# Activation block sums of the feed-forward stage: one piece per product of chunk 1, the rest under the products down of chunk 0, each engine one step further apart

## The chip, the cores and the metric

One core of a Trainium2 chip runs the whole program in one launch. The metric is the device time of that launch in microseconds (us). The engines are TensorE (PE; PEld is its weight load), VectorE (DVE), ScalarE (ACT), GpSimd (POOL) and the sync engine (SP), which issues the DMAs here. Each engine takes its instructions in the order in which the program lists them and waits on semaphores for the others.

## What is computed

Two layers of an encoder, 1024 tokens by 1024 features, in float32. A layer is a mixer (two kinds of attention with gates) and a feed-forward part. Only the feed-forward part matters here:

```python
h = rmsnorm(x, pre_ffn_g[l]) @ w_ffn_up[l]       # 1024 -> 4096
f = jnp.square(jax.nn.relu(h)) @ w_ffn_down[l]   # 4096 -> 1024
x = x + rmsnorm(f, post_ffn_g[l])
```

## The kernel before, in words

**Split operands.** Every float32 operand of a large product is scaled by a power of two and split into a float16 high part and a float16 low part. A product is then three matmuls (high by high, high by low, low by high) that add up in PSUM. ACT makes a high part (a copy into float16) and DVE the low part (value minus high part).

**Chunks.** The 4096 hidden features are worked in 8 chunks of 512. Chunks 0 and 1 are multiplied up directly (`up_first`, `up`). Chunks 2 to 7 (`up7`) use a seven-product scheme for 2 by 2 blocks, which needs five sums or differences of blocks of the activations (`UB` lists seven operands, two of them plain blocks) and sums of blocks of the weights. `down` multiplies a chunk down and adds into `acc`.

**The activation sums.** `u_sums` is a Python generator. It makes the five block sums in two halves each, so ten pieces, numbered 0 to 9 here. One piece is: two additions of 128x1024 on POOL (`tt` with `G`) into a buffer of the pool "p", a third addition on DVE (`tt`), the high part on ACT (`act`) and the low part on DVE (`sub`). Each `next(usums)` is a step of a software pipeline: before the change, step n issues the low part of piece n-2, the third addition and the high part of piece n-1 and POOL's additions of piece n. The pool "p" (`wk()`) has 4 buffers; a sum holds one until its low part is done.

**The order around it.** The part is in a `manual_schedule`: for PE, DVE, ACT and POOL the order in the program is the order on the engine. `run` first makes the second halves of chunk 0 (`up_first(i, 1)`, one step after each of the four), then prepares the low and high parts of chunk 0's hidden values (`split`) and of its down weights (`down_weights`) as work in a queue that `up(1, 6)` takes from: six pieces of it (`adv`) after the matmuls of each of its four products. Before the change a step of `u_sums` stands after the first and after the fourth of these six, and what is left is issued after `up`.

In `up(1, 6)` the four products are called P0 to P3 here, 48 matmuls of 128x512 each. The queue gives: hidden norm (under P0); four high and four low parts of the hidden values and the first square of the down weights (P1); the other three squares and their sum, line 239 (P2); the high and low parts of the down weights (P3). A mark in the queue makes the sum's use, a one-column matmul with a matrix of ones (line 243), stand on PE in front of the next product:

```python
        def stat():

            if mark[0]:
                mark[0] = next(work[0]) == 2
```

`relu2` (two instructions on ACT) empties each product's PSUM; PSUM of this kind (A) has two buffers, so a product needs the one before last emptied.

Then `down(0, 2)` makes eight products of 24 matmuls, one for each block of 128 tokens (tb 0 to 7). After each, DVE empties PSUM into `acc`. Beside them run the head of chunk 2's weights (`up_head`: two DMAs, four squares on ACT that each take a "p" buffer, their sum at line 1287 and its matmul of ones at line 1291, in front of tb 3) and `flow()`, which makes weight sums for `up7(2)`: an addition on POOL into a "p" buffer, a high part on POOL, a low part on DVE.

All of this occurs once in each of the two layers.

Of the kernel before, what the change touches and what calls it, by code (L numbers as in the profile page):

```python
# [44 lines left out]
def tile_hybrid_encoder(  # L45
# [27 lines left out]
    def mt(shape, dt=F16):  # L73
        return sb.tile(shape, dt, tag="m", name=nm("m"), bufs=NM)
# [7 lines left out]
    def wk(shape=(128, 1024), dt=F32):  # L82
        return sb.tile(list(shape), dt, tag="p", name=nm("p"), bufs=NP)

    def gt(shape, dt=F32):
        return sb.tile(shape, dt, tag="g", name=nm("g"), bufs=NG)
# [10 lines left out]
    def lay(n):  # L97
        return sb.tile([128, 4], F32, tag="lay", name=nm("lay"), bufs=32)[:, :n]

    def psA(cols=1024):  # L100
        return ps.tile([128, 1024], F32, tag="A", name=nm("A"), bufs=2)[:, :cols]
# [16 lines left out]
    def ts(o, i, s1, op0, s2=None, op1=None, e=V):  # L118
        if op1 is None:
            e.tensor_scalar(out=o, in0=i, scalar1=s1, scalar2=None, op0=op0)  # L120
        else:
            e.tensor_scalar(out=o, in0=i, scalar1=s1, scalar2=s2, op0=op0, op1=op1)  # L122

    def tt(o, a, b, op, e=V):
        e.tensor_tensor(out=o, in0=a, in1=b, op=op)  # L125
# [4 lines left out]
    def sub(o, a, b, e=V):  # L130
        tt(o, a, b, ALU.subtract, e)
# [4 lines left out]
    def stt(o, a, s, b, op0, op1):  # L136
        V.scalar_tensor_tensor(out=o, in0=a, scalar=s, in1=b, op0=op0, op1=op1)  # L137

    def act(o, i, f=AF.Copy, **k):
        S.activation(o, i, f, **k)  # L140
# [1067 lines left out]
    def ffn(l, U, su_inv, wup0, nxt):  # L1208
# [24 lines left out]
        def u_sums():  # L1233

            homes = iter((gt, gt, ptt, mt, mt))
            items = []
            for i, (a, b, sg) in enumerate(UB):
                if b is None:
                    UC[i] = [[U[*a, e][:, k, :] for k in range(4)] for e in range(2)]
                    continue  # L1240
                home = next(homes)
                if home is gt:
                    t = [[gt([128, 2, 512], F16) for _ in range(2)] for e in range(2)]
                else:
                    full = [home([128, 4, 512]) for e in range(2)]
                    t = [[f[:, 2 * j : 2 * j + 2, :] for j in range(2)] for f in full]
                UC[i] = [[t[e][k // 2][:, k % 2, :] for k in range(4)] for e in range(2)]
                items += [(a, b, ALU.add if sg > 0 else ALU.subtract, t, j) for j in range(2)]
            yield 1
            n0 = len(items)  # L1250
            sums = {}
            for n in range(n0 + 2):
                if n > 1:
                    *_, t, j = items[n - 2]
                    sub(t[1][j], sums.pop(n - 2), t[0][j])
                if 0 < n <= n0:
                    a, b, op, t, j = items[n - 1]
                    ks = slice(2 * j, 2 * j + 2)
                    tt(sums[n - 1], sums[n - 1], U[*b, 1][:, ks, :], op)
                    act(t[0][j], sums[n - 1])  # L1260
                if n < n0:
                    a, b, op, t, j = items[n]
                    ks = slice(2 * j, 2 * j + 2)
                    sums[n] = wk((128, 2, 512))
                    tt(sums[n], U[*a, 0][:, ks, :], U[*b, 0][:, ks, :], op, G)
                    tt(sums[n], sums[n], U[*a, 1][:, ks, :], ALU.add, G)
                yield 1
# [113 lines left out]
        def up_mm(wu, b, f, pa, ths):  # L1381
            (wh,), (wl,) = wu[b][:2]
            for k in range(8):
                for (a, r) in ((0, 0), (0, 1), (1, 0)):
                    lw = (wh, wl)[a][:, k, f * 128 : (f + 1) * 128]
                    for i, th in enumerate(ths):
                        TE.matmul(pa[:, i * 512 : (i + 1) * 512], lw, U[k // 4, th, r][:, k % 4, :],  # L1387
                                  start=(k == 0 and a == 0 and r == 0), stop=(k == 7 and a == 1))

        def up_scale(wu, b):  # L1390
            c = lay(1)
            mul(c, wu[b][2], su_inv)
            return c

        def relu2(h, pa, c, o):
            act(h, pa, AF.Relu, scale=c)
            act(h, h, AF.Square, accum_out=o)
# [17 lines left out]
        def up(ch, n):  # L1415
            wu = wup.pop(ch)
            hf, hs = [], lay(4)
            st[ch] = hf, hs
            for b in range(2):
                c = up_scale(wu, b)  # L1420
                for f in range(2):
                    pa = psA()
                    stat()
                    up_mm(wu, b, f, pa, (0, 1))
                    for i in range(n):
                        adv(1)
                        if i in (0, 3):
                            next(usums, 0)
                    h = mt([128, 1024], F32)
                    relu2(h, pa, c, hs[:, b * 2 + f : b * 2 + f + 1])  # L1430
                    hf.append(h)
            drain()
# [43 lines left out]
        def down_factor(ch, inv):  # L1476
            c = lay(1)
            mul(c, wdn[ch][2], inv)
            wdn[ch].append(c)

        def split_and_weights(ch):

            dw = down_weights(ch, (ptt,) * 4, 2)
            next(dw)
            work.extend([split(ch), dw])
# [42 lines left out]
        def down(ch, n):  # L1528
            down_factor(ch, st.pop((ch, "inv")))
            for tb in range(8):  # L1530
                pa = psA()
                stat()
                down_mm(ch, tb, pa, True, True)
                adv(n)
                if ch < 5 and tb > 0:
                    flow()
                if ch == 0:
                    acc[tb] = mt([128, 1024], F32)
                    ts(acc[tb], pa, wdn[ch][4], ALU.mult)
                else:  # L1540
                    stt(acc[tb], pa, wdn[ch][4], acc[tb], ALU.mult, ALU.add)
            drain()
            if ch < 5:
                for _ in range(8):
                    flow()
            del st[ch], wdn[ch]
# [65 lines left out]
        def run():  # L1612
            nonlocal g_post, usums
            with tc.manual_schedule(engines=ENGINES):
                work.extend([up_weights(1, b, wt) for b in range(2)])
                usums = u_sums()
                for i in range(4):
                    up_first(i, 1)
                    next(usums)
                drain()  # L1620
                split_and_weights(0)
                up(1, 6)
                for _ in usums:
                    pass
                for ch in range(1, 6):
                    work.append(up_head(ch + 1))
                    down(ch - 1, 2)
                    if ch < 5:
                        split_and_weights(ch)
                        up7(ch + 1, (4, 4, 2, 2, 2, 3, 5))  # L1630
                work.append(up_head(7))
                up7(6, (2,) * 7)
                for _ in range(4):
                    flow()
                split_and_weights(5)
                up7(7, (4, 4, 2, 2, 2, 3, 5))
                work.append(last_work())
                down(5, LW)
                g_post = load_gain(post_ffn_g[l], D)
                if not lastl:  # L1640
                    work.append(nxt["start"]())
                for tb in range(7 if lastl else 8):
                    stat()
                    if tb > 2:
                        turn(tb - 3)
                    pa = psA()
                    for ch in (6, 7):
                        down_mm(ch, tb, pa, ch == 6, ch == 7)
                    adv(LA)
                    norms(tb)  # L1650
                    xs[tb] = wk()
                    SY.dma_start(out=xs[tb], in_=x1[l][tb * 128 : (tb + 1) * 128, :])
                    stt(acc[tb], pa, wdn[6][4], acc[tb], ALU.mult, ALU.add)
                    square(acc[tb], nv[tb][:, 0:1])
                    if lastl:
                        mul(acc[tb], acc[tb], g_post, G)
                drain()
                if lastl:
                    last_block()
# [15 lines left out]
        g_post, usums = None, None  # L1675
# [75 lines left out]
    for l in range(depth):  # L1751
        hold, wup0 = {}, [[], []]
        YA, ivA, YB, ivB = mixer(l, U, su_inv, b2u, w1, first if l == 0 else None, late, mid_weights(l, hold), hold)
        gp, _, sf, sf_inv = gain_scale(pre_ffn_g[l], 4)
# [74 lines left out]
```

## Time and profile before

| | us |
|---|---|
| median of 3 runs | 3113.38 |
| lowest, highest | 3111.36, 3116.12 |
| profiled execution, its own time | 3116.08 |
| its span (first to last instruction) | 3114.3 |
| granted TensorE clock, mean share | 0.979 |

The times of the trace are microseconds from the span's start. Layer 0's feed-forward part begins near 900, layer 1's near 2440. Rows of the kernel's helpers carry the helper's line: L125 is an addition or subtraction (`tt`), L137 a `scalar_tensor_tensor` (a low part or a PSUM add), L140 any ACT instruction, L1387 the matmuls up of chunks 0 and 1, L1525 the matmuls down. Buffers go by pool: "g", "pt" and "m" with L140 and L125 on "p" are the pieces of `u_sums`, "A" is PSUM.

### The profile page before, as it was taken

The numbers are of one execution on the slowest core, as the hardware profiler recorded it, in microseconds if no ns is written. First come the engines' busy times: TensorE is split into PE (matmuls) and PEld (weight loads), VectorE is DVE, ScalarE is ACT, GpSimd is POOL, SyncE is SP. The second block draws the span as 40 slices with busy tenths as digits, with TensorE's granted clock in tenths as the row PEclk, the third lists the DMA queues.
The fourth block names the chain that finished last, engine by engine and source line by source line (L and its number), as shares of the span: only waits on it lengthen the run. The fifth ranks groups of instructions, "written<-read, shape, count | busy, mean of one in ns | idle before, by whom it ended". The sixth has DMA issues, their size and how long they took to land. (4 is left out here: it accounts for less than half of the span.)

```text
span 3114.3 us, 45811 instructions
## 1 busy us (share of the span) xinstructions
PE 2902.7 (93%) x17146; PEld 1549.9 (50%) x17146; DVE 2059.8 (66%) x3836; ACT 1521.9 (49%) x2490; POOL 1024.9 (33%) x1261
## 2 busy tenths in 40 slices
PE   7989999897898999999999899998979989999998
PEld 5754555553353444444467445555534434444443
DVE  7687766876657555555776877778866575555655
ACT  4455566675545333324444556576655443333341
POOL 3342344543215222240224323355331252222402
PEclk9999999999999999999999999999989999999999
DMA  4058867879421111112410587677893111111212
GB/s 152 15 115 191 187 157 149 171 176 255 147 82 54 55 55 52 52 40 102 134 56 16 135 186 193 141 177 157 194 269 129 55 41 54 55 55 55 76 66 82
DMA packets 686782, 352.73 MB, mean 113 GB/s; under 512 B 556352, under 2 KB 635744, under 8 KB 686560
## 3 DMA queue, kind: packets, MB, share of 16 engines
q1 hardware_dynamic: 686560, 349.81, 42.6%
q8 instruction: 135, 2.21, 0.3%
q14 instruction: 87, 0.71, 0.1%
HBM read 171.46 MB, written 44.04 MB: 69 GB/s over the span
## 5 line engine op out<-in xcount | busy, mean ns | idle before, releaser
L1525 PE MATMUL A<-pt,m 128*128 128x512 f16 x2484 | 547.5, 381 | 4.5 <-DVE pt L137 2.8
L1525 PEld LDWEIGHTS <-m 128*128 128x128 f16 x3072 | 301.5, 99 | 366.4 <-issue 11.9
L137 DVE SCALAR_TENSOR_TENSOR g<-p,sm,g 128x1024 f16<-128x1024 f32 x256 | 329.4, 1287 | 55.7 <-DMA pt<-g 20.5
L675 PE MATMUL B<-m,w 128*128 128x512 f16 x1536 | 354.5, 380 | 0.2 <-DVE lay L245 0.2
L122 POOL TENSOR_SCALAR g<-p,sm 128x1024 f16<-128x1024 f32 x128 | 148.5, 1160 | 505.0 <-DVE sm L877 354.0
L137 DVE SCALAR_TENSOR_TENSOR m<-A,lay,m 128x1024 f32<-128x1024 f32 x95 | 121.7, 1283 | 207.2 <-PE A L1525 207.2
L140 ACT ACTIVATE m<-m,lay 128x1024 f16<-128x1024 f32 (+2 forms) x148 | 146.4, 1037 | 219.7 <-DVE m L125 189.4
L319 PEld LDWEIGHTS <-m 128*128 128x128 f16 (+1 forms) x1600 | 159.6, 100 | 183.9 <-issue 99.9
L675 PEld LDWEIGHTS <-w 128*128 128x128 f16 x1536 | 146.1, 99 | 169.5 <-issue 12.6
L125 DVE TENSOR_TENSOR m<-B,m 128x512 f16<-128x512 f32 (+3 forms) x208 | 127.5, 635 | 141.7 <-ACT m L140 140.9
L318 PE MATMUL A<-m,m 128*128 128x256 f16 (+3 forms) x448 | 159.8, 357 | 62.3 <-DVE p L137 31.6
L320 PEld LDWEIGHTS <-m 128*128 128x128 f16 (+1 forms) x1600 | 159.3, 100 | 104.9 <-issue 9.1
L318 PEld LDWEIGHTS <-m 128*128 128x128 f16 (+1 forms) x1600 | 160.3, 100 | 98.9 <-issue 11.2
L140 ACT ACTIVATE p<-A,sm,kq 128x1024 f32<-128x1024 f32 x128 | 153.8, 1202 | 114.0 <-DVE p L862 87.7
L319 PE MATMUL A<-m,m 96*128 96x512 f16 (+3 forms) x576 | 209.0, 363 | 0.0
L320 PE MATMUL A<-m,m 96*128 96x512 f16 (+3 forms) x576 | 208.5, 362 | 0.0
L140 ACT ACTIVATE m<-A 128x1024 f32<-128x1024 f32 x24 | 24.5, 1022 | 361.6 <-PE A L320 360.5
L140 ACT ACTIVATE p<-A,sm,lay 128x1024 f32<-128x1024 f32 x128 | 154.3, 1205 | 72.9 <-DVE p L862 55.2
L907 PE MATMUL B<-pt,m 128*64 128x256 f16 x2688 | 175.0, 281 | 14.8 <-DMA pt<-g 14.8
L137 DVE SCALAR_TENSOR_TENSOR w<-st,lay,w 128x1024 f16<-128x1024 f32 (+2 forms) x80 | 131.1, 1643 | 86.0 <-POOL w L122 61.5
L125 POOL TENSOR_TENSOR p<-m,m 128x1024 f32<-128x1024 f16 (+1 forms) x28 | 72.4, 2584 | 341.5 <-ACT m L140 214.3
L125 DVE TENSOR_TENSOR m<-m,A 128x1024 f32<-128x1024 f32 x96 | 113.9, 1218 | 92.3 <-PE A L320 92.3
(201 smaller groups left out, 6555.2 us busy)
## 6 DMA issues: line engine op xcount, KB each, us to landing
st<-in_w_ffn_up_dram SPq DMA_DIRECT2D x32, 1024.0 KB, 5.3
st<-in_w_ffn_down_dram SPq DMA_DIRECT2D x32, 1024.0 KB, 4.8
st<-in_w_in_dram SPq DMA_DIRECT2D x32, 512.0 KB, 3.9
gd<-g SPq DMA_DIRECT2D x64, 256.0 KB, 2.4
p<-gd SPq DMA_DIRECT2D x64, 256.0 KB, 5.2
pt<-g SPq DMA_TRANSPOSE x512, 2.8
ba<-g SPq DMA_DIRECT2D x32, 256.0 KB, 2.4
st<-in_w_o_dram SPq DMA_DIRECT2D x8, 1024.0 KB, 7.2
```

Of the source, the lines that this page charges most:

```text
L122: e.tensor_scalar(out=o, in0=i, scalar1=s1, scalar2=s2, op0=op0, op1=op1)
L125: e.tensor_tensor(out=o, in0=a, in1=b, op=op)
L137: V.scalar_tensor_tensor(out=o, in0=a, scalar=s, in1=b, op0=op0, op1=op1)
L140: S.activation(o, i, f, **k)
L318: TE.matmul(o, lh, rh, start=first, stop=False)
L319: TE.matmul(o, lh, rl, start=False, stop=False)
L320: TE.matmul(o, ll, rh, start=False, stop=last)
L675: TE.matmul(gate_live[g], lw, U[k // 4, th, (0, 1, 0)[v]][:, k % 4, :], start=(i == 0), stop=(i == 23))
L907: TE.matmul(pc[64 * i : 64 * i + 64, :256], VT[:, v, c, vc : vc + 64], PTs[g, i][p][:, c, :], start=(c == 0 and v == 0 and p == 0), stop=( ...
L1525: TE.matmul(pa if pa.shape[1] == 512 else pa[:, n * 512 : (n + 1) * 512], a, r[k // 2][:, k % 2, n * 512 : (n + 1) * 512], start=(first an ...
```

## The change

The steps of `u_sums` get one more stage: the high part on ACT moves from the step of the third addition to the step after it, and the low part to the step after that. In `up` only the fourth of the six `adv` is followed by a step. The steps that are left are issued in `down(0, 2)`, one in each tb after its matmuls and its work from the queue; the loop that issued the rest after `up` moves to the end of `down`, where it finds nothing left.

```diff
@@ u_sums
-            for n in range(n0 + 2):
-                if n > 1:
+            for n in range(n0 + 3):
+                if n > 2:
+                    *_, t, j = items[n - 3]
+                    sub(t[1][j], sums.pop(n - 3), t[0][j])
+                if 1 < n < n0 + 2:
                     *_, t, j = items[n - 2]
-                    sub(t[1][j], sums.pop(n - 2), t[0][j])
+                    act(t[0][j], sums[n - 2])
                 if 0 < n <= n0:
                     a, b, op, t, j = items[n - 1]
                     ks = slice(2 * j, 2 * j + 2)
                     tt(sums[n - 1], sums[n - 1], U[*b, 1][:, ks, :], op)
-                    act(t[0][j], sums[n - 1])
@@ up
-                        if i in (0, 3):
+                        if i == 3:
                             next(usums, 0)
@@ down
                 adv(n)
+                if ch == 0:
+                    next(usums, 0)
                 if ch < 5 and tb > 0:
                     flow()
...
             if ch < 5:
+                for _ in usums:
+                    pass
                 for _ in range(8):
                     flow()
@@ run
                 up(1, 6)
-                for _ in usums:
-                    pass
```

Which step stands where:

| place | steps n before | steps n after |
|---|---|---|
| up_first(1..3, 1) | 0, 1, 2 | 0, 1, 2 |
| P0, P1, P2, P3 | 3 4, 5 6, 7 8, 9 10 | 3, 4, 5, 6 |
| between up and down | 11 | none |
| down, tb 0 to 5 | none | 7, 8, 9, 10, 11, 12 |

## Rows read from the trace of the kernel before

**Rows 1.** The page, part 1: busy time by engine.
```profile
PE 2902.7 (93%) x17146; PEld 1549.9 (50%) x17146; DVE 2059.8 (66%) x3836; ACT 1521.9 (49%) x2490; POOL 1024.9 (33%) x1261
```

**Rows 2.** Waits, 940 to 1045: engine, line, releaser: total us, times, longest.
```profile
PE B L243 <- DVE sm L239: 10.6, 1, 10.6
DVE sm L239 <- ACT pt L140: 3.2, 1, 3.2
```

**Rows 3.** PE in order of time, layer 0: start, length, instructions [idle before].
```profile
947.21 0.28 PE L243 MATMUL B<-sm,ones 128*128 128x1 f32 x2
...
957.70 0.28 PE L1443 MATMUL B<-sm,ones 128*128 128x1 f32 x2
957.84 20.88 PE L1387 MATMUL A<-m,w 128*128 128x512 f16 x96
989.30 0.59 PE L243 MATMUL B<-sm,ones 128*128 128x1 f32 x2 [10.58 <-DVE sm L239]
...
1001.72 15.70 PE L1525 MATMUL A<-pt,m 128*128 128x512 f16 x72
...
1043.30 0.38 PE L318 MATMUL A<-g,w 128*128 128x512 f16 x1
```

**Rows 4.** The same view of layer 1.
```profile
2529.22 0.59 PE L243 MATMUL B<-sm,ones 128*128 128x1 f32 x2 [10.58 <-DVE sm L239]
...
2541.39 15.70 PE L1525 MATMUL A<-pt,m 128*128 128x512 f16 x72
```

**Rows 5.** Stretches of layer 0: us, busy by engine (count), granted clock, DMA.
```profile
978.70:989.30 10.60, 0.02 (x1) 0.00 (x0) 7.40 (x6) 8.31 (x13) 9.21 (x4) 0.69 0.00 0
989.30:1001.70 12.40, 12.39 (x50) 5.53 (x51) 10.14 (x12) 8.32 (x9) 0.77 (x1) 0.85 0.05 11
```

**Rows 6.** ACT in order of time, layer 0.
```profile
962.85 1.06 ACT L140 ACTIVATE g<-p 128x1024 f16<-128x1024 f32 x1 [5.08 <-DVE p L125]
963.81 1.10 ACT L140 ACTIVATE m<-A,lay 128x1024 f32<-128x1024 f32 x1
...
978.59 1.06 ACT L140 ACTIVATE pt<-p 128x1024 f16<-128x1024 f32 x1 [5.43 <-DVE p L125]
...
985.93 1.06 ACT L140 ACTIVATE m<-p 128x1024 f16<-128x1024 f32 x1 [2.02 <-DVE p L125]
...
987.93 1.04 ACT L140 ACTIVATE pt<-st 128x1024 f16<-128x1024 f32 x1
```

**Rows 7.** DVE in order of time, layer 0, chunk 1.
```profile
963.94 1.95 DVE L125 TENSOR_TENSOR g<-p,g 128x1024 f16<-128x1024 f32 x1 [0.61 <-ACT g L140]
965.80 3.15 DVE L125 TENSOR_TENSOR p<-p,m 128x1024 f32<-128x1024 f32 x1
968.88 7.41 DVE L137 SCALAR_TENSOR_TENSOR m<-m,lay,m 128x1024 f16<-128x1024 f32 x3
...
977.35 1.21 DVE L125 TENSOR_TENSOR p<-p,m 128x1024 f32<-128x1024 f32 x1
978.48 3.14 DVE L137 SCALAR_TENSOR_TENSOR m<-m,lay,m 128x1024 f16<-128x1024 f32 x1
...
989.09 0.16 DVE L239 TENSOR_REDUCE sm<-sm 128x1 f32<-128x4 f32 x1 [3.20 <-ACT pt L140]
```

**Rows 8.** POOL in order of time, layer 0.
```profile
929.47 2.12 POOL L125 TENSOR_TENSOR p<-p,m 128x1024 f32<-128x1024 f32 x1
...
961.70 3.10 POOL L125 TENSOR_TENSOR p<-m,m 128x1024 f32<-128x1024 f16 x1
...
967.84 3.10 POOL L125 TENSOR_TENSOR p<-m,m 128x1024 f32<-128x1024 f16 x1
...
1019.36 2.21 POOL L122 TENSOR_SCALAR w<-st,lay 128x1024 f16<-128x1024 f32 x2 [9.23 <-DVE lay L122]
```

**Rows 9.** DVE in order of time, layer 0, under the products down.
```profile
1003.29 1.28 DVE L137 SCALAR_TENSOR_TENSOR pt<-st,lay,pt 128x1024 f16<-128x1024 f32 x1
...
1012.28 1.28 DVE L120 TENSOR_SCALAR m<-A,lay 128x1024 f32<-128x1024 f32 x1 [3.90 <-PE A L1525]
```

## The prediction

> **What bounds the kernel now.** I began with busy time by engine: TensorE is busy for 2902.7 of 3114.3 us, no other engine for more than 66% [rows 1]. So time is won only where TensorE stands idle, and a step that moves between other engines counts only through a TensorE wait. Next I took the waits of the stretch that the change touches. There TensorE has one: 10.6 us, in a single piece, for DVE's line 239 [rows 2]. In TensorE's order of time it stands in front of P3: P2's matmuls end at 978.72 (957.84 + 20.88), the matmul of ones starts at 989.30 [rows 3]; layer 1 has the same gap of 10.58 us [rows 4]. The stretches show a second price. The granted clock is 0.69 in the gap and 0.85 in P3 after it [rows 5], a mix of the two levels, 1.2 and 2.4 GHz. From its matmul of ones on, P3 takes 1001.72 - 989.30 = 12.42 us where P0 took 957.70 - 947.21 = 10.49 [rows 3]. In layer 1 P3 takes 12.17 [rows 4].
>
> **Why TensorE waits.** Going back from 989.09: the sum of line 239 waits 3.20 us for the fourth square [rows 7], which starts at 987.93 behind the high part of piece 6 (985.93, itself 2.02 late for DVE). The high part of piece 5 waited 5.43 us, and ahead of it that of piece 3 waited 5.08 and held up P0's `relu2` to 963.81 [rows 6], though P0 ended at 957.9. Each of these is a high part that the program puts right behind the DVE addition it needs, while DVE is behind: the additions take up to 3.15 us instead of 1.21, three low parts 7.41 instead of 3 x 1.28 [rows 7, 9], because POOL is at work all the time, with a new piece every 967.84 - 961.70 = 6.14 us [rows 8].
>
> **The change, part by part.** It adds and removes no instruction and moves no DMA. It moves steps 7 to 10 out of `up` and puts one more stage between the addition and the high part, and between high and low part.
>
> *ACT up to the sum.* In the new order the high part under P0 is piece 1's, added two steps earlier, so it does not wait. P0's `relu2` can start at the product's end, 957.9, not 963.81. Then come four high parts of the hidden values, piece 2's, one square: at 1.1 us each some 9 us, to 967. P1's `relu2` is bound by P1's end (968.3) and done at 970.6; three squares of 1.13 with their read-out end at 974.0.
>
> *DVE up to the sum.* It has to do four low parts, one piece's low part and addition before the sum, from 961.2 (first high part) on. Undisturbed that is 6 x 1.25 = 7.5 us, to 968.7; at the disturbed prices 7.41 + 1.95 + 3.15 + 3.14 = 15.7 us [rows 7], to 976.9, and some 2 us more if the small multiplication ahead of the sum is disturbed too: 978.9. So the sum is due between 974.2 and 979.1, and TensorE wants it at 978.7: 0 to 0.4 us of wait instead of 10.58. I take 0, since POOL makes one piece per product here and is idle for nearly half of it.
>
> *Down weights under P3.* P2's `relu2` ends at 981, four high parts at 985.4; the last low part stands behind piece 3's low part and piece 5's addition. It ends between 989.6 (all undisturbed) and 993.5 (the disturbed prices), and `down` starts at 989.2. Before, that low part ended 2.85 us after the start (1003.29 + 1.28 against 1001.72) [rows 3, 9] and cost hardly anything. So the price is 0 to 1.5 us a layer; I take 0.
>
> *The first products down.* A product down takes (1043.30 - 1001.72) / 8 = 5.20 us [rows 3]. DVE empties it in 1.28, and before was idle for 3.90 us ahead of it [rows 9]; with two PSUM buffers it may be 5.20 - 1.28 = 3.9 us late before TensorE stops. Now tb 0 to 2 hold a whole piece each, tb 3 to 5 the ends. At the pace that the trace shows with POOL busy, 6.14 us [rows 8], three pieces are 3 x (6.14 - 5.20) = 2.8 us late: inside the 3.9. At the disturbed prices, DVE has 1.95 + 3.15 + 1.28 = 6.4 us in each of tb 0 to 2; with the scale of chunk 2 some 7.1 in tb 3, and it may begin 4 us late because of the last low part: 4 + 3.6 + 1.9 - 3.9 = 5.6 us of waiting. So 0 to 5.6; I take 0, by the pace, which is the row nearest to this mix.
>
> The Trainium skill speaks against this part: SBUF — State Buffer, section SBUF: two separate sides, says that DVE (with two SBUF inputs) and GpSimd share a port pair that is locked for a whole instruction, so that the other blocks. The rows agree in kind (3.15 for 1.21, and POOL 3.10 for 2.12) [rows 7, 8]. A full lock would make a piece's four instructions 2 x 2.12 + 2 x 1.21 = 6.7 us, so 4.5 us late after three and 0.6 us of wait a layer; the sum would then be some 1 us smaller.
>
> *What rides along.* In POOL's queue pieces 7 to 9 now stand ahead of chunk 2's weight sums. Their first high part starts at 1019.36, 24 us before `up7` needs it at 1043.30 [rows 3, 8]; a few us later is covered by the rest. The four squares of `up_head` must go through the one "p" buffer that the sums leave free, once piece 4's low part has ended (at most 995.5): four of 1.13, done by 1000.5, wanted by TensorE ahead of tb 3 at 989.2 + 3 x 5.2 = 1004.8. Hidden, by 4 us. SP's weight loads wait for the low parts of the down weights, as before.
>
> **The sum.** The gap: 10.58 in either layer. The slow P3: 12.42 - 10.49 = 1.93 and 12.17 - 10.49 = 1.68. Together 12.5 + 12.3 = 24.8 us; against it nothing taken. The profiled execution, 3116.08, would take 3091.3; it lies 2.7 above the median of 3113.38, so the forecast for a median is 3088.6, said as 3089 (0.8% faster).
>
> **The rivals.** (1) *Part of it is given back in the products down.* DVE falls behind beside POOL and TensorE waits for an emptied buffer in tb 3 to 6. From the bounds: 1 to 6 us a layer, 3091 to 3101, most likely about 3095. For it speaks that DVE was already busy for 10.14 of the 12.40 us under P3 [rows 5]; against it, the pace. (2) *The wait stays.* Line 239 is late for another reason, such as the landing of the down weights that the squares read: then squares run no earlier, and the time stays at 3113. Against it: the fourth square is held by a high part that waits for DVE, not by a DMA [rows 6]. (3) *Slower.* DVE becomes the bound of the products down. If each of its two-input instructions there met POOL in full (3.15 + 3.15 for the piece, 3.14 for the weight sum's low part, 1.28), a product would take 10.7 us instead of 5.20, in six products 33 us a layer; less the 12.4 won that is 41 us slower in all, 3154. It decides from 7.3 us a product on (5.20 + 12.4 / 6). Against it: POOL has only three pieces to make there, some 18 of 31 us. (4) *The change misses its place*: if the steps ran out before `down`, there would be none under it; with four steps in `up` instead of eight, that can't be.
>
> **How the numbers follow.** The forecast has 0.58, rival 1 has 0.32, rival 2 0.04, rival 3 0.04 and 0.02 is left for a larger gain than the sum. What a measurement of this kernel can tell from no change is about 0.2%, 6 us. All of the forecast, of rival 1 and of the remainder are faster by more than that: 0.92; same 0.04, slower 0.04. The range goes from 3085.5 (the forecast less the spread of the three runs) to 3101, the end of rival 1; rivals 2 and 3 and some of the edges are left out.
>
> **What would show it.** Right: no TensorE wait at line 243 in front of P3, a granted clock of 1.00 through P3, line 239 before P2's end, P0's `relu2` at its product's end, products down 5.2 us apart, `up7` starting 12.4 us earlier. Rival 1: TensorE waits at line 1525 for DVE in tb 3 to 6. Wrong: a wait of several us left at line 243, or `up7` starting late for its pieces.

## The result, and the profile after

Beside the kernel before, the changed kernel took 3096.04 us in the median (3092.78 to 3096.89) against 3114.75; the ratio is 0.9939 with a 95% interval of 0.9922 to 0.9956. It is faster by 0.6%, inside the stated range of 3085.5 to 3101, at the place where rival 1 stood and not where the forecast did: 19 us instead of 24.8.

First TensorE in order of time, layer 0 (start, length, instructions, [idle before and what ended it]):

```profile
945.07 0.28 PE L243 MATMUL B<-sm,ones 128*128 128x1 f32 x2
...
955.71 20.88 PE L1389 MATMUL A<-m,w 128*128 128x512 f16 x96
976.42 0.28 PE L243 MATMUL B<-sm,ones 128*128 128x1 f32 x2
...
986.92 15.70 PE L1527 MATMUL A<-pt,m 128*128 128x512 f16 x72
...
1002.60 15.71 PE L1527 MATMUL A<-pt,m 128*128 128x512 f16 x72
1019.42 5.34 PE L1527 MATMUL A<-pt,m 128*128 128x512 f16 x24 [1.11 <-DVE m L120]
1025.86 5.34 PE L1527 MATMUL A<-pt,m 128*128 128x512 f16 x24 [1.10 <-DVE m L120]
1031.04 0.38 PE L318 MATMUL A<-g,w 128*128 128x512 f16 x1
```

The wait of 10.58 us in front of P3 [rows 3] is gone: P2's matmuls end at 976.59 by the model of their ends, and the matmul of ones is in order behind them. P3 takes 986.92 - 976.42 = 10.50 us, as P0 did, where it took 12.42. In the products down there are two new waits, of 1.11 and 1.10 us, in front of tb 6 and tb 7, both for DVE's emptying of PSUM. Layer 1 repeats it to the hundredth:

```profile
2477.43 0.28 PE L243 MATMUL B<-sm,ones 128*128 128x1 f32 x2
...
2508.78 0.28 PE L243 MATMUL B<-sm,ones 128*128 128x1 f32 x2
...
2551.80 5.34 PE L1527 MATMUL A<-pt,m 128*128 128x512 f16 x24 [1.10 <-DVE m L120]
2558.24 5.34 PE L1527 MATMUL A<-pt,m 128*128 128x512 f16 x24 [1.10 <-DVE m L120]
2563.42 0.38 PE L318 MATMUL A<-g,w 128*128 128x512 f16 x1
```

The stretches that answer to [rows 5] (us, then busy us of PE, PEld, DVE, ACT, POOL with their counts, granted clock, DMA share, GB/s) show P3 at full clock in either layer:

```profile
976.40:986.90 10.50, 10.50 (x51) 4.84 (x50) 7.43 (x10) 7.37 (x8) 3.87 (x2) 1.00 0.31 96
2508.80:2519.30 10.50, 10.50 (x52) 4.84 (x51) 7.48 (x10) 7.37 (x8) 3.88 (x2) 1.00 0.31 96
```

From here on **the stage** is the time from the matmul of ones in front of P0 to the first matmul of `up7`. It was 1043.30 - 947.21 = 96.09 us in layer 0 and 95.84 in layer 1; it is 1031.04 - 945.07 = 85.97 and 85.99. That is 10.1 and 9.9 us won, 20.0 together, against 19.3 by which the two spans differ (3114.3 and 3095.0). The other 0.7 is made of shifts of up to 2.6 us in the mixers, in both directions, where the program is the same; they differ as much between runs of one kernel. So the stage, which repeats to a few hundredths, is the measure of what follows.

ACT and DVE show why the sum of the down weights is in time. These are two rows of ACT and two of DVE, in order of time:

```profile
955.77 1.11 ACT L140 ACTIVATE m<-A,lay 128x1024 f32<-128x1024 f32 x1 [5.27 <-PE A L1389]
...
970.55 1.04 ACT L140 ACTIVATE pt<-st 128x1024 f16<-128x1024 f32 x1
```

```profile
959.14 3.67 DVE L137 SCALAR_TENSOR_TENSOR m<-m,lay,m 128x1024 f16<-128x1024 f32 x3 [2.66 <-ACT m L140]
...
971.71 0.16 DVE L239 TENSOR_REDUCE sm<-sm 128x1 f32<-128x4 f32 x1 [1.56 <-ACT pt L140]
```

P0's `relu2` starts at P0's end, where it had been 6 us behind [rows 6]. The three low parts take 3.67 us, where they took 7.41 [rows 7]. The sum stands at 971.71, 4.9 us before P2 ends (976.59); before, it came 10.4 us after that.

The new waits come from DVE under the products down. Its rows in tb 2 to 5, each emptying (line 120) behind the work of its tb, and POOL's beside them:

```profile
1002.17 3.12 DVE L125 TENSOR_TENSOR p<-p,m 128x1024 f32<-128x1024 f32 x1 [2.02 <-POOL p L125]
1005.22 1.27 DVE L120 TENSOR_SCALAR m<-A,lay 128x1024 f32<-128x1024 f32 x1
...
1008.36 3.37 DVE L125 TENSOR_TENSOR p<-p,m 128x1024 f32<-128x1024 f32 x1
1011.65 1.27 DVE L120 TENSOR_SCALAR m<-A,lay 128x1024 f32<-128x1024 f32 x1
1012.84 2.04 DVE L125 TENSOR_TENSOR m<-p,m 128x1024 f16<-128x1024 f32 x1
1014.80 3.37 DVE L137 SCALAR_TENSOR_TENSOR w<-st,lay,w 128x1024 f16<-128x1024 f32 x1
1018.10 1.27 DVE L120 TENSOR_SCALAR m<-A,lay 128x1024 f32<-128x1024 f32 x1
1019.29 3.26 DVE L125 TENSOR_TENSOR m<-p,m 128x1024 f16<-128x1024 f32 x1
1022.48 2.13 DVE L137 SCALAR_TENSOR_TENSOR w<-st,lay,w 128x1024 f16<-128x1024 f32 x1
1024.54 1.27 DVE L120 TENSOR_SCALAR m<-A,lay 128x1024 f32<-128x1024 f32 x1
```

```profile
996.95 2.13 POOL L125 TENSOR_TENSOR p<-m,m 128x1024 f32<-128x1024 f16 x1 [5.95 <-ACT p L140]
...
1004.29 2.99 POOL L125 TENSOR_TENSOR p<-p,m 128x1024 f32<-128x1024 f32 x1
1007.25 3.40 POOL L125 TENSOR_TENSOR p<-st 128x1024 f32<-128x1024 f32 x1
1010.63 3.18 POOL L122 TENSOR_SCALAR w<-st,lay 128x1024 f16<-128x1024 f32 x2
1013.78 3.31 POOL L125 TENSOR_TENSOR p<-st,st 128x1024 f32<-128x1024 f32 x1
```

The emptying of PSUM (line 120) comes every 6.45 us (1011.65, 1018.10, 1024.54), while a product asks for it every 5.2; before, it came in time, with 3.90 us of idle ahead of it [rows 9]. Between two of them stand a low part of the last pieces (2.04, 3.26) and a low part of chunk 2's weights (3.37, 2.13); undisturbed each takes 1.2 to 1.3 us. POOL has no idle there: its last piece ends at 1007.28 and the weight sums follow at once.

DVE is late before that, in tb 2. Its emptying of tb 1 starts in time, at 997.48; that of tb 2 was due 5.2 us later, at 1002.7, and starts at 1005.22, 2.5 us late. DVE had stood idle for 2.02 us for POOL's sum of piece 8, and its addition then took 3.12 us instead of 1.21. POOL had started that piece only at 996.95, after 5.95 us of idle until the last of the four squares of chunk 2's head, which take "p" buffers too, was done. Tb 3 and tb 4 add 1.2 us each: 5.0 us late at tb 4 (1018.10), 1.1 over the 3.9 that the prediction allows, and TensorE waits 1.11 in front of tb 6. Tb 5 adds as much again, and that is the wait in front of tb 7.

### The profile page after: what moved, and what is told of

Read it like the earlier page. It is cut to its first block, busy times and chain, and to the rows that moved or that the text cites. A ratio compares the mean times of both kernels' runs of the same rounds, so it can differ in the third digit from the quotient of the medians.

```text
span 3095.0 us, 45817 instructions
## 1 busy us (share of the span) xinstructions
PE 2901.7 (94%) x17146; PEld 1549.6 (50%) x17146; DVE 2069.1 (67%) x3836; ACT 1523.8 (49%) x2490; POOL 1030.2 (33%) x1261
```

## The experiments

What they add up to, the stage in us; the last two columns are the median of the timed runs and the ratio to the kernel before on the same chip:

| kernel | layer 0 | layer 1 | TensorE waits in the stage, a layer | median | ratio (95%) |
|---|---|---|---|---|---|
| before | 96.09 | 95.84 | 10.58 at P3 | | |
| changed | 85.97 | 85.99 | 1.1 + 1.1, tb 6, 7 | 3096.04 | 0.9939 (0.9922 to 0.9956) |
| places only | 83.43 | 83.43 | none | 3095.01 | 0.9927 (0.9908 to 0.9946) |
| stages only | 95.34 | 95.32 | 7.30 at P3, 2.5 in tb 0 | 3109.63, one run | |
| weight sums late | 83.43 | 83.43 | none | 3089.30 | 0.9906 (0.9885 to 0.9927) |
| steps one place earlier | 83.43 | 83.42 | none | 3092.74 | 0.9920 (0.9900 to 0.9939) |
| changed, again | 85.98 | 85.96 | 1.1 + 1.1 | 3098.62 | 0.9938 (0.9926 to 0.9951) |
| places only, again | 83.43 | 83.42 | none | 3094.08 | 0.9926 (0.9912 to 0.9939) |
| no weight additions | 83.43 | 83.43 | none | 3100.45, one run | |
| steps one place later | 87.90 | 90.38 | 3.96 at tb 6 | 3101.54, one run | |
| POOL at half load (old places) | 88.29 | 89.77 | 2.91 at P3 | 3101.80, one run | |

**Places or stages.** Two kernels with one half of the change each. The first has the new places and the old two-stage order of `u_sums`:

```diff
-            for n in range(n0 + 3):
...
+            for n in range(n0 + 2):
+                if n > 1:
+                    *_, t, j = items[n - 2]
+                    sub(t[1][j], sums.pop(n - 2), t[0][j])
                 if 0 < n <= n0:
...
                     tt(sums[n - 1], sums[n - 1], U[*b, 1][:, ks, :], op)
+                    act(t[0][j], sums[n - 1])
```

> The new places of the steps (one per product in chunk 1, the rest under the products down of chunk 0), with the two-stage order of before: a piece's high part stands in the same step right behind its addition on DVE. The stage is measured from the matmul of ones in front of P0 to the first matmul of up7: 96.0 us before, 86.0 changed. Theory A (the places do it: half the load per product is enough): no TensorE wait at line 243 in front of P3, stage 85 to 87, whole time within 3 us of the changed kernel. Theory B (the extra stage does it, because a high part right behind its addition holds up ACT): ACT waits for DVE in every step as before, the sum of line 239 is late, a wait of 2 to 6 us stays, stage 88 to 93.

The stage is 83.43 us in both layers: no wait in front of P3, and none in the products down either. Theory A holds, and more than it asked for: without the extra stage the kernel wins 12.7 and 12.4 us a layer, all of the 24.8 us forecast for the change as a whole. DVE is still without a pause there. Its order of time from the emptying of tb 3 to that of tb 5:

```profile
1013.87 1.27 DVE L120 TENSOR_SCALAR m<-A,lay 128x1024 f32<-128x1024 f32 x1
1015.07 2.03 DVE L125 TENSOR_TENSOR m<-p,m 128x1024 f16<-128x1024 f32 x1
1017.03 3.37 DVE L137 SCALAR_TENSOR_TENSOR w<-st,lay,w 128x1024 f16<-128x1024 f32 x1
1020.32 1.27 DVE L120 TENSOR_SCALAR m<-A,lay 128x1024 f32<-128x1024 f32 x1
1021.51 3.27 DVE L137 SCALAR_TENSOR_TENSOR w<-st,lay,w 128x1024 f16<-128x1024 f32 x1
1024.70 1.27 DVE L120 TENSOR_SCALAR m<-A,lay 128x1024 f32<-128x1024 f32 x1
```

In this run `down` started at 990.53, so tb 4 ended near 990.53 + 5 x 5.2 = 1016.5 and its PSUM may be emptied from 1020.4 at the latest (3.9 later). It starts at 1020.32: the kernel is at the edge. The last piece's low part (1015.07) stands ahead of it; from there on only a weight sum's low part is left for each product, and DVE comes round after 4.38 us and recovers. In the changed kernel the last low part of a piece stands one product later, in tb 5. Its DVE is also later from tb 2 on: by 2.5 us at the emptying of tb 2, which is 1.1 us late here (1007.44, with that of tb 0 in time at 995.91). Its piece 8 starts on POOL 10.0 us after `down`, here 6.8: with the extra stage a sum holds its "p" buffer one step longer, the first square waits 1.81 us for the low part of piece 4, and piece 8 stands behind the squares. No run parts these two effects of the extra stage. By the rows, 1.4 us less at tb 2 would take the wait at tb 6 away and leave that at tb 7 (an estimate).

The second kernel is the changed one with the old places and the new order:

```diff
-                        if i == 3:
+                        if i in (0, 3):
                             next(usums, 0)
...
-                if ch == 0:
-                    next(usums, 0)
...
                 up(1, 6)
+                for _ in usums:
+                    pass
```

> The old places (two steps per product, the rest after up), with the three-stage order. Theory A: POOL and DVE are still loaded with two pieces per product, the wait in front of P3 stays at 7 us or more, stage 92 or longer. Theory B: ACT no longer waits behind DVE's additions, the wait falls below 4 us, stage 86 to 90.

TensorE in order of time, layer 0:

```profile
986.26 0.59 PE L243 MATMUL B<-sm,ones 128*128 128x1 f32 x2 [7.30 <-DVE sm L239]
...
999.66 4.04 PE L1527 MATMUL A<-pt,m 128*128 128x512 f16 x18 [0.69 <-DVE pt L137]
1005.52 11.38 PE L1527 MATMUL A<-pt,m 128*128 128x512 f16 x52 [1.81 <-DVE pt L137]
```

The wait falls only from 10.58 to 7.30, and the low parts of the down weights are now late for the first product down, 0.69 and 1.81 us. The stage wins 0.75 and 0.52 us. Theory B falls: with two pieces per product the extra stage is worth next to nothing.

**The two new waits.** Two kernels take the overlap of the last pieces with chunk 2's weight sums apart, one from either side:

```diff
-                if ch < 5 and tb > 0:
+                if ch < 5 and tb > (4 if ch == 0 else 0):
                     flow()
```

> The changed kernel, with chunk 2's weight sums (flow) only from tb 5 of the products down of chunk 0 on. Theory C (the two waits of 1.1 us in front of tb 6 and tb 7 come from the weight sums meeting the last pieces on POOL and DVE): both waits go, stage 83.8, some 4 us less in all than the changed kernel. Rival D (the pieces alone make DVE late): the waits stay in part, stage 85 to 86. Rival E (the weight sums are then too late for up7): waits of TensorE in the first products of up7 take their place, and the whole time is not shorter.

```diff
                 usums = u_sums()
+                next(usums)
                 for i in range(4):
```

> The changed kernel, with every step of the activation sums one place earlier (the first step that issues work stands after up_first(0, 1)), so the products down hold the pieces in tb 0 to 4, not 0 to 5. Theory C: the overlap of pieces and weight sums shrinks by one tb, at most one wait of about 1 us is left, stage 83.8 to 85. Rival D: DVE falls behind by the same amount one product earlier, stage 86.

Both waits go in both kernels, the stage is 83.43: theory C. Tb 2 is still 2.5 and 2.8 us late there (emptied at 1008.47 and 1004.50), so that lateness alone costs nothing; it takes the pieces and the weight sums behind it to pass the 3.9. The late weight sums pay a little of it back as rival E would have it, one wait of 1.00 us a layer at line 1445, in front of the second product of `up7`, behind DVE's line 1440. The earlier steps have no such wait.

The other way round, the steps were put one place later, by leaving out the one under P0:

```diff
-                        if i == 3:
+                        if i == 3 and (b or f):
                             next(usums, 0)
```

> The changed kernel with no step under P0, so every later step is one place later and the pieces end in tb 6 instead of tb 5. Theory C (the overlap of pieces and weight sums is the price): more waits than two, 3 to 5 us a layer, stage 86.5 to 88.5. Rival H (the price is the extra stage as such, wherever it ends): the same two waits of about 1.1 us, one product later, stage 86.0.

A wait of 3.96 us stands in front of tb 6 in layer 0 and of 3.97 in layer 1, nearly twice the 2.2 of the changed kernel. Tb 4 holds the low part and the addition of a piece and a weight sum's low part there, and its emptying comes 9.50 us after that of tb 3 (1010.81, 1020.31). So the waits follow from where the pieces end: none with the last low part in tb 4, 2.2 us with tb 5, 4 us with tb 6. Theory C's size held for layer 0 (87.90); layer 1 came out at 90.38, above it, because the clock fell there (below).

**What lengthens DVE's instructions.** POOL's additions of weight blocks for chunk 2 were left out, with all of DVE's instructions kept:

```diff
-                if b:
+                if b and ch != 2:
                     t = wk()
```

> The changed kernel without POOL's five additions of weight blocks for chunk 2 (the first block alone is used, so the result is another; DVE has as many instructions as before). Theory F (DVE is late because POOL's additions lengthen its two-input instructions): these fall to 1.2 to 2.1 us in tb 3 to 6, no wait, stage 83.4. Rival G (DVE has too many instructions in tb 3 to 5, whatever POOL does): the waits of 1.1 us stay, stage 85.5 to 86.

DVE in order of time, tb 2 to 5:

```profile
1011.78 1.21 DVE L125 TENSOR_TENSOR p<-p,m 128x1024 f32<-128x1024 f32 x1
1012.91 1.27 DVE L120 TENSOR_SCALAR m<-A,lay 128x1024 f32<-128x1024 f32 x1
1014.11 1.95 DVE L125 TENSOR_TENSOR m<-p,m 128x1024 f16<-128x1024 f32 x1
1015.98 2.13 DVE L137 SCALAR_TENSOR_TENSOR w<-st,lay,w 128x1024 f16<-128x1024 f32 x1
1018.04 1.27 DVE L120 TENSOR_SCALAR m<-A,lay 128x1024 f32<-128x1024 f32 x1
1019.23 1.21 DVE L125 TENSOR_TENSOR m<-p,m 128x1024 f16<-128x1024 f32 x1
```

The same addition takes 1.21 us instead of 3.37, the low parts 1.21 to 2.13 instead of 2.04 to 3.37, and both waits are gone. Theory F: it is POOL beside DVE, not the number of DVE's instructions. (The whole time of this one run, 3100.45 us, says nothing against it: from one stage to the next it took 1449.2 us, against 1440.7 to 1447.2 in the other runs here.)

The rows also say what kind of disturbance it is. DVE's 3.37 us for 1.21 is a wait of 2.16, about one POOL addition (2.12 undisturbed [rows 8]), and the instructions that read PSUM (line 120, 1.27 us) are not lengthened in any of these rows. That fits the lock of a whole instruction that the Trainium skill describes on the page SBUF — State Buffer, section SBUF: two separate sides; the traces agree, with 3.37 and 1.21. The 6.7 us a piece that the prediction worked out from a full lock of all four instructions is above what the rows show: 6.14 [rows 8], and 5.15 from piece 8 to piece 9 on POOL in the changed kernel.

**What the old wait was.** The kernel before, with the second of POOL's two additions of each piece left out:

```diff
                     tt(sums[n], U[*a, 0][:, ks, :], U[*b, 0][:, ks, :], op, G)
-                    tt(sums[n], sums[n], U[*a, 1][:, ks, :], ALU.add, G)
                 yield 1
```

> The kernel before (old places, two stages) with POOL's second addition of each of the ten pieces left out, so POOL has half the work in chunk 1 while DVE and ACT have the same instructions in the same order (the result is another). Theory J (the old wait was POOL's load: it lengthens DVE's instructions and paces the pieces at 6.1 us): the wait in front of P3 falls from 10.6 us to at most 2, stage 83.4 to 86. Rival K (it was the number of pieces per product in the queues of DVE and ACT, whatever POOL does): the wait stays at 6 us or more, stage 91 or longer.

TensorE in order of time (a row of each layer), the stretches of the wait in layer 0 and of P3 in both layers, and a row each of DVE and ACT ahead of the wait:

```profile
981.04 0.38 PE L243 MATMUL B<-sm,ones 128*128 128x1 f32 x2 [2.91 <-DVE sm L239]
...
2514.84 0.59 PE L243 MATMUL B<-sm,ones 128*128 128x1 f32 x2 [2.92 <-DVE sm L239]
```

```profile
978.10:981.00 2.90, 0.03 (x1) 0.00 (x0) 0.17 (x2) 2.70 (x5) 1.51 (x1) 1.00 0.00 0
981.00:993.30 12.30, 12.26 (x50) 5.34 (x51) 10.05 (x13) 8.31 (x9) 0.00 (x0) 0.86 0.10 25
2514.80:2528.60 13.80, 13.76 (x50) 5.90 (x51) 11.55 (x14) 8.74 (x10) 0.00 (x0) 0.76 0.20 58
```

```profile
964.64 5.31 DVE L137 SCALAR_TENSOR_TENSOR m<-m,lay,m 128x1024 f16<-128x1024 f32 x3
972.25 1.06 ACT L140 ACTIVATE pt<-p 128x1024 f16<-128x1024 f32 x1 [3.55 <-DVE p L125]
```

This lies between the two theories: 7.7 of the 10.6 us go with half of POOL's work, 2.9 stay. In the wait itself ACT is busy for 2.70 of 2.90 us and DVE hardly at all. But ACT had been idle for 3.55 us before, for an addition on DVE, whose three low parts still took 5.31 us beside POOL (3.67 in the changed kernel). So what stays is ACT's queue with two pieces, the squares and `relu2` in one product, or what half of POOL's work still holds up; the run doesn't part them. The stage missed theory J's 83.4 to 86 chiefly by P3's clock, which fell after a wait of 2.9 us as it did after 10.6.

**Places only beside the changed kernel.** Both kernels once more, beside the kernel before on one chip:

> The changed kernel once more, beside the next kernel and the kernel before on one chip. Stage 86.0 in both layers with the two waits of 1.1 us; whole time 19 to 20 us under the kernel before (ratio about 0.9937).

> The new places with the two-stage order (as e1_places_only), timed beside the changed kernel. Theory A2 (the extra stage costs 2 x 2.55 us, since it ends the pieces one product later and brings nothing in chunk 1): 24 to 25 us under the kernel before, 4 to 6 under the changed kernel. Theory B2 (the stage lengths don't add up to the whole, or the difference is lost further on): within 2 us of the changed kernel.

The medians are 3098.62 and 3094.08 us beside 3118.24 of the kernel before: 19.6 and 24.2 under it, 4.5 apart. Theory A2 holds; by the stages 2 x 2.55 = 5.1 were due. The intervals of the two ratios overlap (0.9926 to 0.9951 and 0.9912 to 0.9939), so the whole times alone lean that way, and the stages, which repeat to 0.03 us, decide it. So the new places with the old two stages are faster than both, by the stage. The changed kernel with the steps one place earlier, or with the later weight sums, has the same stage; between these three the whole times don't decide.

## Why the prediction was right, and where not

**The gap in front of P3: right.** It was priced at 10.58 us a layer and taken to go to 0, with bounds of 0 to 0.4; it went to 0. The sum of line 239, put between 4.5 us before P2's end and 0.4 after it, came 4.9 before. **The slow P3: right.** Priced at 1.93 and 1.68 us; P3 takes 10.50 in both layers at a granted clock of 1.00, which gives back 1.92 and 1.67.

**Why TensorE waited: half right.** The prediction gave two reasons, a high part that the program puts right behind the addition it needs, and DVE late because POOL is always at work. The second is shown: half of POOL's work less, and 7.7 of the 10.6 us are gone (POOL was not at work quite all the time: ahead of piece 8, at 977.57, it was itself idle for 3.56 us for DVE). The first counts for less: with the high part right behind its addition (places only) there is no wait at all, and with a stage between them at the old load 3.3 us of the wait go, 7.30 stay, and 2.5 come back in tb 0.

**Down weights under P3: right.** 0 to 1.5 us a layer, taken as 0: no wait in tb 0 to 2.

**The products down: the step that failed.** "So 0 to 5.6; I take 0, by the pace, which is the row nearest to this mix." The products down take 1031.04 - 986.92 = 44.12 us, before 41.58: a loss of 2.54 us a layer, 5.1 in all. That is the whole of what is missing, 24.8 forecast against 20.0 found, and 0.3 more, which the part up to `down` won beyond its price. The sum by the pace counts three pieces, 2.8 us of lateness in tb 0 to 2, and stops there; tb 3 to 5, where the ends of the pieces meet the weight sums of chunk 2, it put at nothing. The lateness after tb 2 was 2.5 us, so that term came out near its size, but by luck: POOL's pieces 8 and 9 follow each other at 5.15 us, not 6.14, and what made DVE late was the idle of 2.02 us for piece 8, which had to wait for the squares' buffer, and one addition of 3.12 us. What was missing is 1.2 us for each of tb 3 to 5, in which DVE needs 6.45 us: 2.5 + 3 x 1.25 - 3.9 = 2.4 us of waiting, near the 2.2 seen. The disturbed price of a product, 6.4 us, was the right one there; the upper bound of 5.6 also charged it to tb 0 to 2, with 4 us for the last low part of the down weights. The 0.6 us that the prediction worked out for a full lock stops at three pieces as well.

**Rival 1: this is what happened**, at 2.5 us a layer of the 1 to 6 named, at tb 6 and 7, for DVE's emptying of PSUM, as it said. Its whole time of "most likely about 3095" is 1 us from the 3096 measured. Rival 2 (the wait stays) and rival 3 (DVE as the bound, over 7.3 us a product) did not occur; DVE reached 6.45. What rides along was hidden as said: `up7` starts without a wait for its pieces, and the four squares end at 996.9, 5.6 us before TensorE wants their sum at 1002.46. What they did not leave alone is piece 8, which was not priced.

**The profile, step by step.** No wait at line 243, clock 1.00 in P3, `relu2` at the product's end: all seen. Products down 5.2 us apart: for six of eight. `up7` earlier by 12.4 us in its stage: by 10. Of the range, the lower end does not come out of its own numbers: the forecast less the spread of the three runs is 3088.6 - 4.8 = 3083.8, not 3085.5. The measured 3096 lies far from it.

## What to carry to other kernels

Spreading background work over more of a matmul stream can win the whole of a stall, but price it with everything that meets it at its new place, at the disturbed durations, until the last low part is done, and not with the pace of the work by itself. A deeper software pipeline ends one place later for every stage added, and holds its buffers one place longer; where the end of the pipeline meets the next job's start, that can cost more than the slack it brings, so run the move without the extra stage as well. A double-buffered PSUM forgives one product's time less the emptying (here 3.9 us): take that as the budget of lateness and add up DVE's time product by product against it.

## What was not expected of the hardware

The price of a TensorE pause in granted clock did not follow its length. After 10.6 us P3 took 1.9 and 1.7 us longer; after 2.9 us 1.8 in layer 0 and 3.3 in layer 1 (12.29 and 13.76 against 10.49). With the steps one place later, the same pause of 3.97 us was followed by full clock in layer 0 and by a mean of 0.78 in layer 1, where two products took 13.18 us against 10.70 (stretches from the end of the pause to `up7`):

```profile
1021.64:1032.34 10.70, 10.68 (x48) 4.67 (x48) 10.70 (x7) 0.00 (x0) 10.70 (x5) 1.00 0.01 2
2556.70:2569.88 13.18, 13.18 (x49) 5.33 (x48) 12.73 (x7) 0.00 (x0) 13.18 (x6) 0.78 0.00 0
```

A pause of 1.1 us, as in the changed kernel, cost nearly nothing beyond itself (2.54 us a layer for two pauses of 2.2 together). So a pause of 3 or 4 us may cost nearly as much again, or nothing: these runs don't say what decides it.
